# Second block's tokens in reverse order, and the keys of both blocks in one matrix, in a two-layer hybrid decoder kernel

## The chip, the cores and the metric

The kernel runs on one core of one Trainium2 chip. The metric is the device time of one execution in microseconds (us); the time before is the median of three runs. A profiled execution is one more run, with the hardware profiler on; all rows below are from it. The engines are named as the profile names them: PE is TensorE's matmuls, PEld its weight loads, DVE is VectorE, ACT is ScalarE, POOL is GpSimd, SP is SyncE.

## The reference

The input is 256 tokens of width 1024, all in fp32. Layer 0 mixes the tokens with a gated linear recurrence, HGRN2, of 8 heads of 128; layer 1 mixes them with attention. Each is followed by a SwiGLU network of width 2816, each sub-layer has an RMS norm ahead of it and a residual add behind it, and a last RMS norm closes the trunk.

```python
# layer 0, per head: S_t = diag(f_t) S_{t-1} + (1 - f_t) i_t^T ; o_t = S_t^T q_t
q = jax.nn.silu(q); f = lbf + (1.0 - lbf) * jax.nn.sigmoid(fz); k = 1.0 - f
...
diff = cum[:, :, :, None, :] - cum[:, :, None, :, :]          # cum: running sum of log f
decay = jnp.exp(jnp.where(causal[:, :, None], diff, -jnp.inf))
scores = jnp.einsum('bhtn,bhsn,bhtsn->bhts', qb, kb, decay)
...
# layer 1 (256 tokens are one block, so every query sees its own block, causally)
s_own = jnp.einsum('bhqd,bhpd->bhqp', qb, kown).astype(f32) * scale + bias_own
s_own = jnp.where(dist_own >= 0, s_own, -jnp.inf)
```

The weight of key s in query t is a product of the gates f between them, feature by feature, so it is no single matrix product. `bias_own` is a table looked up by the bucket of the distance between query and key.

## The kernel before

**Weights and activations in two parts.** A product of fp32 accuracy is made of three products in TensorE's single-pass format fp32r: weight and activation are each split in a high and a low part (hi = rounded, lo = the rest), and hi·hi, lo·hi and hi·lo are summed in PSUM (`mm_w`, `mm_x`). Weights come from HBM in 206 loads (line 399, issued from SP's queue) into a ring of six buffers `raw`; ScalarE writes `whi` (line 410) and VectorE writes `wlo` (line 412), each into a ring of six pieces of up to 1024 columns. Products whose operands aren't split are fp32 matmuls, which stand as two records each in the trace. Every `mm` is recorded with the helper's line 453.

**Order.** The order of instructions on each engine is made by a planner (`Order`) when the program is built: each step has an engine, an estimated cost, a due time and the steps that it needs. TensorE's main stream, the products with weights, is written out in order; the small matmuls of the heads ("T" steps) are put into it where the planner believes their inputs to have been ready for 1500 ns. The hardware's semaphores then make sure of the real order.

**The heads of layer 0.** The class `Core` does one head: `forget` makes the gates f, `query` makes q, and `step(m)` for m = 1, 2, 4 ... 64 builds the tree of products of gates: at level m, the tokens stand in pairs of runs of m, and the queries of each second run are multiplied with the product of the gates of their run so far (`Q[2m]`), the keys of each first run with the product of what follows them (`K[2m]`). With m from 2 to 32, each has one multiplication on VectorE (lines 848 and 853; 840 for the first queries) and a copy of the untouched half on ScalarE (850, 855; 843). `scores` then multiplies keys and queries level by level on TensorE: at level m, keys of the first runs meet queries of the second runs. The 256 tokens are two blocks of 128 (index a). For m = 4, 8 and 16, `level` makes one fp32 matmul for each block: the block's whole key matrix `K[m]` of 128 less m columns is the stationary operand, and the 64 queries of the second runs are the moving one. Level 32 and level 64 share two matmuls (`both`), for which the copies on lines 862 and 864 bring the operands together; one more (`k128`, `q128`) joins the two blocks. `s0` does level 2 and the diagonal's neighbours, and a product with `ones128` the diagonal. VectorE copies the blocks that count from PSUM to the score matrix `pm`, by a mask (`take`, line 890, and `s0e`, line 912), and ScalarE those of the large levels (`far`, lines 941 to 945). `values` multiplies `pm` with the values.

**The bias table.** Behind the heads, one fp32 matmul of 33 rows and 384 columns (`tbr`, `oh`) spreads the table of biases over distances; the result goes to DRAM (`scr`), and 8 DMAs on POOL's queue (line 1012) bring it back as `bt`, one row of 256 biases per query and head, read in layer 1's attention (`attend`). The POOL queue also makes the inverse norms (`ny`, line 609).

## Time and profile before

| | us |
|---|---|
| median of 3 runs | 619.15 |
| the runs | 618.98 to 620.29 |
| the profiled execution | 618.95 |
| its span, first to last instruction | 617.2 |
| PE busy | 609.3 (99%) |
| PEld busy | 589.1 (95%) |
| DVE busy | 441.9 (72%) |
| ACT busy | 361.4 (59%) |

Busy time is the time that at least one instruction of the engine was under way. Matmuls are pipelined, so a single matmul's duration in a timeline is longer than what it adds to the time; that is read from the distances between the starts. The granted clock of TensorE is 0.997 of full speed over the execution.

### The profile page before, as it was taken

How to read it: one execution, taken by the hardware profiler on the slowest of the kernel's cores; microseconds unless marked ns; L12 is line 12 of the kernel's file. 1: busy time of each engine (PE TensorE's matmuls, PEld its weight loads, DVE VectorE, ACT ScalarE, POOL GpSimd, SP SyncE). 2: the span in 40 equal slices, each digit the busy share in tenths (PEclk: the TensorE clock that was granted, in tenths of full speed). 3: DMA queues.
4: the chain of work that ended last, by engine and by line, in shares of the span. 5: the costliest groups of instructions: out<-in, count | busy, mean ns of one | idle time of the engine just before them, and what ended most of it. 6: DMA issues, size and time to landing. Idle time of an engine off the chain costs nothing.

```text
span 617.2 us, 12450 instructions
## 1 busy us (share of the span) xinstructions
PE 609.3 (99%) x4856; PEld 589.1 (95%) x4856; DVE 441.9 (72%) x798; ACT 361.4 (59%) x705; POOL 45.8 (7%) x84
## 2 busy tenths in 40 slices
PE   9999999999999999999999999999999999999995
PEld 7899999999999999999998899999999999999995
DVE  6899888869676666666669678877686666666654
ACT  7798887857554444444447566655674444444443
POOL 0042223201300000000000000000100000000003
PEclk9999999999999999999999999999999999999998
DMA  8856534443985555555563564446645666555501
GB/s 308 326 172 197 172 104 142 143 162 116 224 290 202 180 199 198 186 198 198 182 202 118 217 212 148 161 138 204 202 151 196 204 202 184 190 189 178 184 2 69
DMA packets 32951, 111.82 MB, mean 181 GB/s; under 512 B 4395, under 2 KB 5836, under 8 KB 32892
## 3 DMA queue, kind: packets, MB, share of 16 engines
q1 hardware_dynamic: 31340, 108.82, 53.3%
q0 software_dynamic: 448, 1.25, 1.0%
q10 hardware_dynamic: 1104, 0.95, 0.6%
q8 instruction: 38, 0.62, 0.4%
q14 instruction: 21, 0.17, 0.1%
HBM read 109.76 MB, written 1.25 MB: 180 GB/s over the span
## 4 chain that ended last, share of the span: by engine, by line
PE 99%; DVE 0%; ACT 0%; issue 0%; POOL 0%; POOLq 0%; ACTq 0%
PE psB L453 49%; PE psA L453 49%; PE psB L1169 0%; PE psB L1215 0%; PE psA L614 0%; DVE fw L1268 0%; ACT raw L1279 0%; DVE raw L1246 0%; PE psB L614 0%; ACT sq L1249 0%; POOL ident masks.py:199 0%; DVE fa L1273 0%; POOL ident masks.py:197 0%; DVE fz L1274 0%; DVE fz L1270 0%
## 5 line engine op out<-in xcount | busy, mean ns | idle before, releaser
L412 DVE TENSOR_TENSOR wlo<-raw,whi 128x1024 fp32r<-128x1024 f32 (+1 forms) x208 | 248.9, 1206 | 105.8 <-ACT whi L410 105.5
L410 ACT ACTIVATE whi<-raw 128x1024 fp32r<-128x1024 f32 (+1 forms) x207 | 213.9, 1046 | 143.9 <-issue 66.2
L453 PE MATMUL psB<-xh,whi 128*128 128x256 f32 x608 | 171.2, 285 | 0.0
L453 PE MATMUL psB<-xh,wlo 128*128 128x256 f32 x608 | 166.6, 277 | 0.0
L453 PE MATMUL psB<-xl,whi 128*128 128x256 f32 x608 | 162.3, 278 | 0.0
L453 PE MATMUL psA<-xh,whi 128*128 128x256 f32 x544 | 150.3, 280 | 0.0
L453 PE MATMUL psA<-xh,wlo 128*128 128x256 f32 x544 | 148.7, 277 | 0.0
L453 PE MATMUL psA<-xl,whi 128*128 128x256 f32 x544 | 144.0, 277 | 0.0
L453 PEld LDWEIGHTS psB<-xh,wlo 128*128 128x128 f32 x608 | 114.5, 188 | 0.8
L453 PEld LDWEIGHTS psB<-xh,whi 128*128 128x128 f32 x608 | 114.5, 188 | 0.8
L453 PEld LDWEIGHTS psB<-xl,whi 128*128 128x128 f32 x608 | 111.4, 188 | 0.0
L453 PEld LDWEIGHTS psA<-xh,whi 128*128 128x128 f32 x544 | 102.2, 188 | 0.6 <-issue 0.5
L453 PEld LDWEIGHTS psA<-xh,wlo 128*128 128x128 f32 x544 | 102.3, 188 | 0.0
L453 PEld LDWEIGHTS psA<-xl,whi 128*128 128x128 f32 x544 | 99.3, 188 | 0.0
L453 PE MATMUL psB<-hl,whi 128*128 128x256 f32 x160 | 44.2, 276 | 0.0
L453 PE MATMUL psB<-hh,whi 128*128 128x256 f32 x160 | 44.2, 276 | 0.0
L453 PE MATMUL psB<-hh,wlo 128*128 128x256 f32 x160 | 44.2, 276 | 0.0
L1028 ACT ACTIVATE u<-sgq 128x256 f32<-128x256 f32 x44 | 18.0, 409 | 36.9 <-DVE sgq L1026 36.7
L453 PE MATMUL psA<-whi,hl 128*128 128x512 f32 (+1 forms) x96 | 36.0, 375 | 0.0
L453 PE MATMUL psA<-wlo,hh 128*128 128x512 f32 (+1 forms) x96 | 35.8, 373 | 0.0
L453 PE MATMUL psA<-whi,hh 128*128 128x512 f32 (+1 forms) x96 | 35.5, 370 | 0.0
L453 PEld LDWEIGHTS psB<-hh,whi 128*128 128x128 f32 x160 | 30.0, 188 | 0.0
(192 smaller groups left out, 807.3 us busy)
## 6 DMA issues: line engine op xcount, KB each, us to landing
raw<-in_w_dram SPq DMA_DIRECT2D x202, 512.0 KB, 3.5
hT<-in_x_dram SPq DMA_DIRECT2D x8, 128.0 KB, 5.3
raw<-in_w_dram SPq DMA_DIRECT2D x4, 256.0 KB, 4.3
bt<-scr POOLq DMA_DIRECT2D x8, 128.0 KB, 7.8
out_dram<-raw SPq DMA_DIRECT2D x2, 320.0 KB, 2.3
bt<-in_final_dram ACTq DMA_DIRECT2D x1, 512.0 KB, 5.3
out_dram<-raw ACTq DMA_DIRECT2D x2, 192.0 KB, 2.3
scr<-be POOLq DMA_DIRECT2D x1, 192.0 KB, 2.5
```

Source lines behind the costliest of these rows:

```text
L410: od.op("A", ca(n), lambda h=h, r=r, o=o, n=n: A.activation(h[:, :n], r[:, o:o + n], AF.Copy), reads=[r], alloc=[h], due=due)
L412: od.op("V", cv(n), lambda h=h, lo=lo, r=r, o=o, n=n: V.tensor_tensor(lo[:, :n], r[:, o:o + n], h[:, :n].bitcast(FT), op=OP.subtract), rea ...
L453: T.matmul(o, a, b, start=start, stop=stop, skip_group_check=True)
L1028: od.op("A", ca(S), lambda: A.activation(sg.tile, gs.tile, AF.Sigmoid), reads=[gs], alloc=[sg], due=due)
```

## The change

Three things are changed.

**The order of tokens.** The host puts tokens 128 to 255 in reverse order, for all of the kernel, and turns the output back. In the second block, the earlier run of each pair then stands second. Two helpers, `first` and `second`, pick the earlier and later runs of both blocks in one access (`cut` writes the access pattern out), and the masks follow.

**Keys of both blocks in one matrix.** At each level only the keys of the earlier runs are wanted, 64 in each block of 128. In the reversed order those of the second block stand where the first block has those that aren't wanted, so the two sets fill one matrix of 128 columns without moving a key to another row of the scores. The decayed keys are kept in one buffer `kk` in place, and ScalarE gathers from it the 128 columns of `K[2m]` at each level. `level` becomes one fp32 matmul with 128 stationary and 128 moving columns, and levels 32 and 64 use it too; the copies of lines 862 and 864 go, `last` has three activations for four, `far` has seven for five.

**The bias table in the reversed order.** It has 640 columns for 384, made by four fp32r matmuls of 33 rows from a split table; `bt` has three blocks of 128 biases for each head, brought back by 18 DMAs on POOL's queue: 2 of 64 partitions and 16 of 16 partitions, in runs of 128 floats where runs of 256 floats were. So that it fits, `so`, `xsf`, `q128`, `k128` and `pm`, which had tiles of their own, now lie inside `bt`'s tile.

```diff
+NOH = 640
...
-    bt = new("bt", [P, NH * S])
+    bt = new("bt", [P, NH * 3 * P])
...
+    def inside(tag, c0, n, bufs):
+        turn = [0]
+        def make():
+            turn[0] += 1
+            c = c0 + n * ((turn[0] - 1) % bufs)
+            return bt.tile[:, c:c + n]
+        rings[tag] = Ring(make, bufs)
+        return c0 + n * bufs
+    at = inside("so", 0, S, 3)
+    at = inside("xsf", at, S, 3)
+    at = inside("q128", at, P, 2)
+    at = inside("k128", at, P, 2)
+    pm_at = at
...
-    oh = fixed("oh", [33, 384])
+    oh = fixed("oh", [33, NOH])
...
-    pms = [fixed(f"pm{i}", [P, 3, P]) for i in range(2)]
+    pms = [Buf(None) for _ in range(2)]
+    for i, t in enumerate(pms):
+        t.tile = bt.tile[:, pm_at + 3 * P * i:pm_at + 3 * P * i + 3 * P].rearrange("p (a t) -> p a t", a=3)
...
-            self.K = {m: new(f"k{m}", [P, S], 2) for m in (2, 4, 8, 16, 32, 64)}
+            self.K = {m: new(f"k{m}", [P, S], 2) for m in (2, 4, 8, 16, 32)}
+            self.K[64], self.kk = new("k128", [P, P], 2), new("k64", [P, S], 2)
...
-                od.op("V", cv(P), lambda: V.tensor_tensor(v4(kn)[:, :, 0], v4(k)[:, :, 0], bc(1), op=OP.mult),
-                      reads=[k, tot], alloc=[kn], due=due)
-                o = od.op("A", ca(P), lambda: A.activation(v4(kn)[:, :, 1], v4(k)[:, :, 1], AF.Copy), reads=[k],
-                          writes=[kn], due=due + .1)
-                o.deps.append(kn.writers[0])
-                if m == 32:
-                    v2 = lambda t: t.tile.rearrange("p (a x) -> p a x", a=2)
-                    od.op("A", ca(64), lambda: A.activation(v2(k)[:, :, 96:128], v2(kn)[:, :, 0:32], AF.Copy), reads=[kn],
-                          writes=[k], due=due + .2)
-                    od.op("A", ca(P), lambda: A.activation(
-                        q.tile.rearrange("p (a y z x) -> p a y z x", a=2, y=2, z=2)[:, :, :, 0],
-                        v2(qn)[:, :, 64:128].rearrange("p a (y x) -> p a y x", y=2), AF.Copy), reads=[qn], writes=[q],
-                        due=due + .2)
...
+                kk, kn = self.kk, K[2 * m]
+                if m == 2:
+                    od.op("V", cv(P), lambda: V.tensor_tensor(first(kk, m), first(k, m), bc(1), op=OP.mult),
+                          reads=[k, tot], alloc=[kk], due=due)
+                    o = od.op("A", ca(P), lambda: A.activation(second(kk, m), second(k, m), AF.Copy), reads=[k],
+                              writes=[kk], due=due + .1)
+                    o.deps.append(kk.writers[0])
+                else:
+                    od.op("V", cv(P), lambda: V.tensor_tensor(first(kk, m), first(kk, m), bc(1), op=OP.mult),
+                          reads=[kk, tot], writes=[kk], due=due)
+                od.op("A", ca(P), lambda: A.activation(
+                    kn[:, :P].rearrange("p (b z i) -> p b z i", z=2, i=2 * m),
+                    cut(kk, 0, (4 * m, 32 // m), (P + 2 * m, 2), (1, 2 * m)), AF.Copy), reads=[kk], alloc=[kn], due=due + .2)
                 return
...
-            self.q128, self.k128 = q, k = new("q128", [P, P], 2), new("k128", [P, P], 2)
-            Q, K = Q[64], K[64]
+            self.q128 = q = new("q128", [P, P], 2)
+            Q, k = Q[64], self.kk
             def last():
-                A.activation(q[:, 64:], Q[:, 192:], AF.Copy, scale=tot[:, 2:3])
-                A.activation(q[:, :64], Q[:, P:192], AF.Copy)
-                A.activation(k[:, :64], K[:, :64], AF.Copy, scale=tot[:, 1:2])
-                A.activation(k[:, 64:], K[:, 64:P], AF.Copy)
-            od.op("A", 4 * ca(64) + 186, last, reads=[Q, K, tot], alloc=[q, k], due=due)
+                A.activation(q[:, :64], Q[:, P:192], AF.Copy, scale=tot[:, 3:4])
+                A.activation(q[:, 64:], Q[:, 192:], AF.Copy)
+                A.activation(k[:, :64], k[:, :64], AF.Copy, scale=tot[:, 1:2])
+            od.op("A", 3 * ca(64) + 186, last, reads=[Q, k, tot], writes=[k], alloc=[q], due=due)
...
+            def take(m, src):
+                d = ((2 * m, 64 // m), (1, m))
+                V.copy_predicated(cut(pm, m, (S - m, 2), *d), cut(mk, moff[m], (64, 2), (m, 64 // m), (1, m)), src)
             def level(b, c, m):
-                o = Q[m].tile.rearrange("p (a b z m) -> p a b z m", a=2, z=2, m=m)[:, :, :, 1]
-                for a in range(2):
-                    mm(b[:P - m, c + 64 * a:c + 64 * a + 64], K[m][:, a * P:a * P + P - m], o[:, a], start=True, stop=True)
+                mm(b[:, c:c + P], K[m][:, :P], second(Q[m], m), start=True, stop=True)
...
             for i, m in enumerate((4, 8, 16)):
-                o = od.op("T", 2 * ct(64), lambda m=m, i=i: level(b, P * i, m), reads=[K[m], Q[m]], due=due,
+                o = od.op("T", ct(P), lambda m=m, i=i: level(b, P * i, m), reads=[K[m], Q[m]], due=due,
                           **(dict(writes=[b]) if i else dict(alloc=[b])))
                 o.deps += [o1] if i else []
                 o1 = o
...
-            b3 = bank("A")
-            def both():
-                for a in range(2):
-                    c = slice(a * P, a * P + P)
-                    mm(b3[:, c], K[32][:, c], Q[32][:, c], start=True, stop=True)
-            o2 = od.op("T", 2 * ct(P), both, reads=[K[32], Q[32]], alloc=[b3], due=due)
-            o3 = od.op("T", ct(P), lambda: mm(b3[:, 2 * P:3 * P], self.k128.tile, self.q128.tile, start=True, stop=True),
-                       reads=[self.k128, self.q128], writes=[b3], due=due)
-            o3.deps.append(o2)
+            b3, o1 = bank("A"), None
+            for i, m in enumerate((32, 64)):
+                o = od.op("T", ct(P), lambda m=m, i=i: level(b3, P * i, m), reads=[K[m], Q[m]], due=due,
+                          **(dict(writes=[b3]) if i else dict(alloc=[b3])))
+                o.deps += [o1] if i else []
+                o1 = o
+            o3 = od.op("T", ct(P), lambda: mm(b3[:, 2 * P:3 * P], self.kk[:, :P], self.q128.tile, start=True, stop=True),
+                       reads=[self.kk, self.q128], writes=[b3], due=due)
+            o3.deps.append(o1)
...
             def far():
-                v = b3[:, :2 * P].rearrange("p (a x) -> p a x", a=2)
-                w = b3[:, :2 * P].rearrange("p (a y z x) -> p a y z x", a=2, y=2, z=2)[:, :, :, 0]
-                to = pm[:, 0:3:2, 64:128].rearrange("p a (y x) -> p a y x", y=2)
-                A.activation(pm[0:32, 0:3:2, 32:64], v[0:32, :, 32:64], AF.Copy)
-                A.activation(pm[64:96, 0:3:2, 96:128], v[64:96, :, 96:128], AF.Copy)
-                A.activation(to[32:64], w[32:64], AF.Copy)
-                A.activation(to[0:32], w[96:128], AF.Copy)
+                for r, n, a, t, c in ((0, 32, 0, 32, 0), (64, 32, 0, 96, 32), (32, 32, 2, 0, 64), (96, 32, 2, 64, 96),
+                                      (0, 64, 0, 64, P), (64, 64, 2, 0, 192)):
+                    A.activation(pm[r:r + n, a, t:t + n], b3[r:r + n, c:c + n], AF.Copy)
                 A.activation(pm[:, 1, :], b3[:, 2 * P:3 * P], AF.Copy)
-            od.op("A", 680, far, reads=[b3], writes=[pm], due=due)
+            od.op("A", 1500, far, reads=[b3], writes=[pm], due=due)
...
+    first = lambda b, m: cut(b, 0, (P + m, 2), (2 * m, 64 // m), *[(1, m)][:m - 1])
+    second = lambda b, m: cut(b, m, (P - m, 2), (2 * m, 64 // m), *[(1, m)][:m - 1])
...
-    scr = dr.tile([P, 384], FT, name="scr")
...
-    e = new("be", [P, 384])
-    eb = bank("B")
-    tbr = new("tbr", [33, P])
-    od.op("A", ca(P), lambda: A.activation(tbr.tile.rearrange("b (h r) -> b h r", r=REP),
-                                           tb.tile.unsqueeze(2).to_broadcast([33, NH, REP]), AF.Copy),
-          reads=[tb], alloc=[tbr], due=80)
-    od.op("T", ct(384), lambda: mm(eb[:, :384], tbr.tile, oh.tile, start=True, stop=True), reads=[tbr, oh], alloc=[eb], due=80)
-    od.op("A", ca(384), lambda: A.activation(e.tile, eb[:, :384], AF.Copy), reads=[eb], alloc=[e], due=80)
-    od.op("G", 1000, lambda: G.dma_start(scr, e.tile), reads=[e], writes=[scr_b], nbytes=196608, due=80)
-    for a in range(P // REP):
-        od.op("G", 1000, lambda a=a: G.dma_start(
-            bt[REP * a:REP * a + REP, :].rearrange("p (h s) -> p h s", h=NH),
-            bass.AP(tensor=scr.tensor, offset=scr.offset + 127 - REP * a, ap=[[383, REP], [REP * 384, NH], [1, S]])),
-            reads=[scr_b], writes=[bt], nbytes=131072, due=90)
+    e = new("be", [P, NOH])
+    ebs = bank("B"), bank("B")
+    tbh, tbl, ohr = new("tbh", [33, P], 1, FR), new("tbl", [33, P], 1, FR), new("ohr", [33, NOH], 1, FR)
+    many = tb.tile.unsqueeze(2).to_broadcast([33, NH, REP])
+    heads = lambda t: t.rearrange("b (h r) -> b h r", r=REP)
+    od.op("A", ca(P), lambda: A.activation(heads(tbh.tile), many, AF.Copy), reads=[tb], alloc=[tbh], due=80)
+    od.op("V", cv(P), lambda: V.tensor_tensor(heads(tbl.tile), many, heads(tbh.tile.bitcast(FT)), op=OP.subtract),
+          reads=[tb, tbh], alloc=[tbl], due=80)
+    od.op("A", ca(NOH), lambda: A.activation(ohr.tile, oh.tile, AF.Copy), reads=[oh], alloc=[ohr], due=80)
+    for eb, c0, n in zip(ebs, (0, 384), (384, NOH - 384)):
+        def biases(eb=eb, c0=c0, n=n):
+            mm(eb[:, :n], tbh.tile, ohr[:, c0:c0 + n], start=True)
+            mm(eb[:, :n], tbl.tile, ohr[:, c0:c0 + n], stop=True)
+        od.op("T", 500, biases, reads=[tbh, tbl, ohr], alloc=[eb], due=80)
+        al = dict(writes=[e]) if c0 else dict(alloc=[e])
+        od.op("A", ca(n), lambda eb=eb, c0=c0, n=n: A.activation(e[:, c0:c0 + n], eb[:, :n], AF.Copy), reads=[eb],
+              due=80, **al)
+    od.op("G", 1000, lambda: G.dma_start(scr, e.tile), reads=[e], writes=[scr_b], nbytes=4 * P * NOH, due=80)
+    heads3 = lambda r, n, j: bt[r:r + n, :].rearrange("p (h j s) -> p h j s", h=NH, j=3)[:, :, j]
+    rows = lambda off, step, n: bass.AP(tensor=scr.tensor, offset=scr.offset + off, ap=[[step, n], [REP * NOH, NH], [1, P]])
+    for r in range(0, P, 64):
+        od.op("G", 1000, lambda r=r: G.dma_start(heads3(r, 64, 1), rows(r, 1, 64)), reads=[scr_b], writes=[bt],
+              nbytes=262144, due=90)
+    for r in range(0, P, REP):
+        for j, off in ((0, 255), (2, 511)):
+            od.op("G", 1000, lambda r=r, j=j, off=off: G.dma_start(heads3(r, REP, j), rows(off - r, NOH - 1, REP)),
+                  reads=[scr_b], writes=[bt], nbytes=65536, due=90)
...
-        parts = ((0, slice(0, P), slice(h * S + P, h * S + S)), (1, slice(P, 384), slice(h * S, h * S + S)))
+        parts = ((0, slice(0, P), slice(h * 384, h * 384 + P)), (1, slice(P, 384), slice(h * 384 + P, h * 384 + 384)))
...
-    for i in range(384):
...
+    for i in range(NOH):
+        dist = 255 - i if i < 384 else i - 511
...
```

## Rows read from the trace of the kernel before

**Rows 1.** the profile's page: span, busy engines, the chain that ended last

```profile
span 617.2 us, 12450 instructions
...
PE 609.3 (99%) x4856; PEld 589.1 (95%) x4856; DVE 441.9 (72%) x798; ACT 361.4 (59%) x705; POOL 45.8 (7%) x84
...
PE 99%; DVE 0%; ACT 0%; issue 0%; POOL 0%; POOLq 0%; ACTq 0%
```

**Rows 2.** waits of TensorE over the whole span: us in total, times, longest

```profile
PE psA L453 <- POOL ident masks.py:199: 1.4, 1, 1.4
```

**Rows 3.** timeline of TensorE near 108 us: start us, us, line, operation

```profile
108.15 0.28 PE L453 MATMUL psB<-xl,whi 128*128 128x256 f32 x1
108.27 0.39 PE L453 MATMUL psA<-q,k 128*128 128x128 f32 x2
...
108.61 0.28 PE L453 MATMUL psB<-xh,wlo 128*128 128x256 f32 x1
108.73 0.28 PE L453 MATMUL psB<-xl,whi 128*128 128x256 f32 x1
108.85 0.54 PE L453 MATMUL psA<-q,k 128*124 128x64 f32 x4
...
109.40 0.28 PE L453 MATMUL psB<-xh,wlo 128*128 128x256 f32 x1
```

**Rows 4.** the same timeline near 101 us

```profile
101.08 0.28 PE L453 MATMUL psB<-xl,whi 128*128 128x256 f32 x1
101.19 0.38 PE L453 MATMUL psA<-q,ones 128*128 128x128 f32 x2
101.41 0.53 PE L453 MATMUL psA<-q,k 128*120 128x64 f32 x4
...
101.96 0.28 PE L453 MATMUL psB<-xh,wlo 128*128 128x256 f32 x1
```

**Rows 5.** the same timeline near 115 us

```profile
114.81 0.28 PE L453 MATMUL psB<-xl,whi 128*128 128x256 f32 x1
114.92 0.51 PE L453 MATMUL psA<-q,k 128*112 128x64 f32 x4
...
115.45 0.28 PE L453 MATMUL psB<-xh,wlo 128*128 128x256 f32 x1
```

**Rows 6.** a group of matmuls, 30 to 130 us: count, busy us, mean ns

```profile
L453 PE MATMUL psA<-q,k 128*124 128x64 f32 x32 | 4.3, 258 | 0.0
```

**Rows 7.** the same timeline near 149 us

```profile
148.44 0.28 PE L453 MATMUL psA<-xh,wlo 128*128 128x256 f32 x1
148.65 0.91 PE L453 MATMUL psB<-oh,tbr 33*128 33x384 f32 x2
...
149.71 0.29 PE L453 MATMUL psA<-xh,wlo 128*128 128x256 f32 x1
```

**Rows 8.** groups of ScalarE (ACT), 30 to 140 us: busy us, mean ns

```profile
L855 ACT ACTIVATE k<-k 128x128 f32<-128x128 f32 x40 | 12.2, 305 | 0.0
...
L862 ACT ACTIVATE k<-k 128x64 f32<-128x64 f32 x8 | 1.9, 242 | 0.0
...
L941 ACT ACTIVATE pm<-psA 32x64 f32<-32x64 f32 x8 | 1.7, 210 | 6.3 <-PE psA L453 5.9 <-DVE pm L890 0.4
```

**Rows 9.** busy time of each engine from 69 to 117 us

```profile
69.00:117.00 48.00, 48.00 (x413) 47.66 (x413) 40.42 (x103) 40.58 (x137) 11.85 (x28) 1.00 0.38 125
```

**Rows 10.** instructions on tile hT: ns min/median/max, first and last start us

```profile
L557 ACT ACTIVATE xh<-hT,pv x32: 491/494/512, 3.6 to 431.7; 128x256 fp32r<-128x256 f32 x32
...
L536 SPq DMA_DIRECT2D hT<-in_x_dram x8: 328/431/730, 0.7 to 10.1; - x8
```

**Rows 11.** line 399's loads, issue to landing, 150 to 172 us

```profile
DMA to landing us min/median/max: 4.7/10.1/13.2
```

**Rows 12.** the same, 180 to 260 us

```profile
DMA to landing us min/median/max: 3.1/3.3/4.3
```

**Rows 13.** timeline of ScalarE near 171 us, in brackets what ended its idle time

```profile
171.15 1.07 ACT L410 ACTIVATE whi<-raw 128x1024 fp32r<-128x1024 f32 x1 [0.34 <-PE psA L453]
```

More of the change, by code (lines that the diff above doesn't have):

```diff
@@ L312, in hybrid_trunk, with cut @@
     rings = {}
+    def cut(b, off, *dims):
+        t = b.tile if hasattr(b, "ring") else b
+        return bass.AP(tensor=t.tensor, offset=t.offset + off, ap=[list(t.ap[0])] + [list(d) for d in dims])
     def ring(tag, shape, bufs, dt=FT):
@@ L775, in forget @@
             k1, k2 = self.k1, self.K[2]
-            fz = lambda z: f.tile.rearrange("p (t z) -> p z t", z=2)[:, z]
-            od.op("A", ca(P), lambda: A.activation(k1[:, :P], fz(0), AF.Identity, scale=-1.0, bias=1.0), reads=[f],
-                  alloc=[k1], due=7)
-            od.op("A", ca(P), lambda: A.activation(k2.tile.rearrange("p (t z) -> p z t", z=2)[:, 1], fz(1), AF.Identity,
-                                                   scale=-1.0, bias=1.0), reads=[f], alloc=[k2], due=7)
+            od.op("A", ca(P), lambda: A.activation(k1[:, :P].rearrange("p (a t) -> p a t", a=2), first(f, 1), AF.Identity,
+                                                   scale=-1.0, bias=1.0), reads=[f], alloc=[k1], due=7)
+            od.op("A", ca(P), lambda: A.activation(second(k2, 1), second(f, 1), AF.Identity, scale=-1.0, bias=1.0),
+                  reads=[f], alloc=[k2], due=7)
             for m in (1, 2, 4, 8, 16, 32):
@@ L843, in step @@
[L843 to L845 removed]
+                    of = lambda z: cut(q, 64 * z, (448 - P * z, 2), (2, 32), (1, 2))
                 else:
                     q, qn = Q[m], Q[2 * m]
[L848 to L849 removed]
@@ L857, in step @@
[L857 to L867 removed]
+                    of = lambda z: (first, second)[z](q, m)
@@ new lines, in step @@
+                od.op("V", cv(P), lambda: V.tensor_tensor(second(qn, m), of(1), bc(0), op=OP.mult), reads=[q, tot],
+                      alloc=[qn], due=due)
+                o = od.op("A", ca(P), lambda: A.activation(first(qn, m), of(0), AF.Copy), reads=[q], writes=[qn],
+                          due=due + .1)
+                o.deps.append(qn.writers[0])
+                kk, kn = self.kk, K[2 * m]
[8 more added lines that the diff above has]
+                          reads=[kk, tot], writes=[kk], due=due)
@@ L913, in s0e @@
                                   mk[:, :2 * P].rearrange("p (a z x) -> p a z x", a=2, z=2), v)
-            od.op("V", cv(P), lambda: take(b0, 0, 2, 192), reads=[b0, mk], writes=[pm], due=due)
+            od.op("V", cv(P), lambda: take(2, cut(b0, 64, (192, 2), (2, 32), (1, 2))), reads=[b0, mk], writes=[pm], due=due)
             b, o1 = bank("A"), None
             for i, m in enumerate((4, 8, 16)):
-                o = od.op("T", 2 * ct(64), lambda m=m, i=i: level(b, P * i, m), reads=[K[m], Q[m]], due=due,
+                o = od.op("T", ct(P), lambda m=m, i=i: level(b, P * i, m), reads=[K[m], Q[m]], due=due,
                           **(dict(writes=[b]) if i else dict(alloc=[b])))
@@ L920, in scores @@
                 o1 = o
-                od.op("V", cv(P), lambda m=m, i=i: take(b, P * i, m), reads=[b, mk], writes=[pm], due=due)
-            od.op("T", ct(P), lambda: mm(b0[:, :384].rearrange("p (a x) -> p a x", a=2)[:, :, :64], ones128,
-                                         ev[:, :P].rearrange("p (a x) -> p a x", a=2), start=True, stop=True),
-                  reads=[ev], writes=[b0], due=due)
+                od.op("V", cv(P), lambda m=m, i=i: take(m, cut(b, P * i, (64, 2), (m, 64 // m), (1, m))), reads=[b, mk],
+                      writes=[pm], due=due)
@@ L925, in scores @@
+            od.op("T", ct(P), lambda: mm(cut(b0, 0, (320, 2), (1, 64)), ones128, ev[:, :P].rearrange("p (a x) -> p a x", a=2),
+                                         start=True, stop=True), reads=[ev], writes=[b0], due=due)
             od.op("V", cv(S), s0e, reads=[b0, mk], writes=[pm], due=due)
-            b3 = bank("A")
-            def both():
-                for a in range(2):
-                    c = slice(a * P, a * P + P)
-                    mm(b3[:, c], K[32][:, c], Q[32][:, c], start=True, stop=True)
@@ L1331, in _constants @@
     pair = np.arange(64)[None]
-    m = [np.concatenate([s == 2 * pair, s // 2 == pair] * 2, axis=1).astype(np.float32)]
+    m = [np.concatenate([s == 2 * pair, s // 2 == pair, s // 2 == pair, s == 2 * pair + 1], axis=1).astype(np.float32)]
     for lv in LEVELS:
-        t = np.arange(P).reshape(-1, 2, lv)[:, 1].reshape(1, -1)
-        ok = ((s // (2 * lv)) == (t // (2 * lv))) & ((s // lv) % 2 == 0)
-        m.append(np.tile(ok.astype(np.float32), (1, 2)))
+        block = np.arange(64)[None] // lv
+        m += [((s // (2 * lv) == block) & ((s // lv) % 2 == a)).astype(np.float32) for a in range(2)]
     return onehot, np.concatenate(m, axis=1).astype(np.uint8)
```

68 lines of the change are left out of this document (24 added, 44 removed).

## The prediction

> **What bounds the kernel now.** Read first the page's engines and its chain: TensorE is under way for 609.3 of 617.2 us, and the chain that ended last is 99% TensorE [rows 1]. A busy TensorE need not be one without waits, so its list of waits comes next: over the whole span it holds one wait, 1.4 us for the identity matrix at the start [rows 2]. So the time is the sum of what TensorE's instructions add to its stream, and an edit counts by the TensorE time that it takes out or puts in, or by a wait that it creates. Busy durations don't give that sum, since matmuls overlap; distances between starts do. In the timeline, products with split weights follow each other at 0.12 us (108.61 to 108.73) [rows 3]. The work of VectorE and ScalarE is hidden as long as they keep ahead: from 69 to 117 us, in the heads, they are busy 40.42 and 40.58 of 48 us, with the granted clock at 1.00, the 2.4 GHz level [rows 9].
>
> **The change, part by part.** The sum is made against the profiled execution: 618.95 us, that is a span of 617.2 and 1.75 us around it, which nothing here touches. The three runs' median is 0.20 above it, and I add that at the end.
>
> *Merged levels 4, 8 and 16.* A small group's price is the distance from the last regular product before it to the second one behind it, less two regular steps of 0.12. One fp32 matmul of 128 stationary and 128 moving columns: 108.15 to 108.61, 0.46 - 0.24 = 0.22 us. The two 64-column matmuls of level 4 (four records): 108.73 to 109.40, 0.67 - 0.24 = 0.43 [rows 3]. Level 8 stands behind a 128-column one: 101.08 to 101.96, 0.88 - 0.24 - 0.22 = 0.42 [rows 4]. Level 16: 114.81 to 115.45, 0.64 - 0.24 = 0.40 [rows 5]. So a matmul with 64 moving columns costs 0.20 to 0.215 us, nearly what one with 128 costs; and as the price falls from level 4 to 16 while the stationary matrix shrinks from 124 to 112 columns and the moving one stays at 64, I read the stationary side as what sets it. The pair becomes one 128 by 128 matmul, for which I take 0.22. Its moving operand has short runs, as the pairs' had, and they didn't make those dearer. Per head: 0.43 + 0.42 + 0.40 - 3 x 0.22 = 0.59 us. There are 8 heads (32 records of level 4, four a head [rows 6]), so 8 x 0.59 = 4.7 us off TensorE's stream. Bounds: if moving columns set the price, the merged matmul costs what the pair cost and nothing is saved; at the cheapest row, 0.20, it is 8 x (1.25 - 0.60) = 5.2.
>
> A rule of the Trainium skill speaks against this part: "TensorE: Matmul & The Clock Gate", section "Back-to-back issue gap", gives about 60 cycles for a matmul of up to 64 columns and 134 for one of 128, so two halves would cost no more than the whole and the gain would be nil. The rows just read, 0.22 for the whole against 0.40 to 0.43 for two halves, disagree, for these fp32 matmuls with a fresh stationary matrix each.
>
> *Levels 32 and 64.* Two 128 by 128 matmuls before (`both`), two after (`level` twice): nothing on TensorE. `s0`, the diagonal, the product of the blocks and `values` keep their number and shapes.
>
> *The bias product.* Its fp32 matmul spans 148.44 to 149.71, 1.27 - 0.24 = 1.03 us [rows 7]. After: two fp32r products of 384 columns and two of 256. With 0.12 for 256 columns and half as much again for 384, 2 x 0.18 + 2 x 0.12 = 0.60, so 0.4 us off. As no row shows an fp32r product of 33 rows, I bound it from 0 to 0.6.
>
> *ScalarE and VectorE in the heads.* On VectorE the number and size of instructions stay. ScalarE: five copies of the untouched keys a head (305 ns each), with line 862 (242, 64 columns) and line 864 (128 columns, so some 305), become one such copy and five gathers; `last` loses one 64-column copy (about 242); `far` has six small activations of at most 64 columns for four, and its smallest takes 210 now [rows 8]. That is 5 x 305 + 242 + 305 against 6 x 305, then 242 less, then at most 2 x 210 more: about -60 ns a head, so nothing. The heads' stage is 5% shorter for TensorE (0.59 of some 11.9 us: 72 regular steps of 0.12, the 1.25 above, and nine more units of 128 columns at 0.22), which lifts both engines from 84% to some 89% of it [rows 9]. Their cover is the stock of split weights, below.
>
> *The added waits.* The next level's multiplication writes `kk` in place, so it waits on VectorE until ScalarE has gathered from `kk`; behind it stand the other steps of the heads and the weight splits of line 412. Before, it waited for ScalarE's copy of the other half, which is as long a step [rows 8]. Chain for chain: one multiplication and one ScalarE copy a level, before and after. I take 0, and from -0.1 to +3 us for the whole, as priced in the rivals. Four kinds of buffers now share one tile. One tile's slices don't wait for each other here: `hT` is loaded in 8 parts until 10.1 us, and ScalarE reads its first part at 3.6 [rows 10]. So 0 for that too.
>
> *POOL's queue and the bias table.* 18 DMAs for 8, 1.5 MB for 1.05, in 3072 runs of 512 B for 1024 runs of 1 KB. POOL has nothing else that is urgent but `ny`, which the planner puts ahead by its due time. What the DMAs disturb are the weights: loads issued from 150 to 172 us take 10.1 us to land (13.2 at most), against 3.3 later [rows 11, 12]. Still TensorE doesn't feel it, since at 171.15 us the split of the next weights waits for TensorE to give a buffer back [rows 13]: the ring is full. Five of six pieces ahead are 5 x 8 x 3 x 0.12 = 14 us of products; less some 3.5 us for a split (1.07 on ScalarE [rows 13], about as much on VectorE, and the waits between), landing may be some 10 us later still before TensorE runs dry. By bytes (1.5 times the delay of 13.2 - 3.3 = 9.9) landing is 5 us later, by runs (3 times) 20 later. I take the former's side: 0; the latter is the slower rival.
>
> "DMA: Bandwidth & Descriptors", section "How a descriptor splits into AXI transactions", in the Trainium skill, has a transfer that starts off a 256 B boundary pay for one more partial transaction; for runs of 512 B in place of 1 KB that would make my estimate some 1.7 times the delay in place of 1.5, which the 10 us still cover. No row shows such runs.
>
> Sum: 618.95 - 4.7 - 0.4 = 613.85, and with the 0.20 to the median **614.0 us**.
>
> **The rivals.**
>
> *Nothing gained by merging.* If moving columns set a merged matmul's price, only 0.4 us goes: 619.15 - 0.4 = 618.7. For it: no row has a 128-column moving operand in runs of 4 to 16 elements. Against it: the prices read in [rows 3 to 5]. 6%. The page on TensorE named above would give this one.
>
> *Waits in the heads.* The planner puts a small matmul where it believes the inputs ready; with VectorE and ScalarE at 89% it may be wrong more often. Ahead of the bias product TensorE already starts 148.65 - 148.44 - 0.12 = 0.09 us late [rows 7]. Nine such groups a head, 8 heads, at 0.09 are 6.5 us at worst; at half of them 3 us, 614.0 + 3 = 617. For it: the longer queue on two engines. Against it: not one wait of TensorE there now [rows 2]. 12%.
>
> *The biases' DMAs starve the weights (slower).* If the delay of the weight loads goes by runs, landing is 20 us later than now where 10 are covered, so TensorE stands still for some 10 us at about 175 to 190 us: 614.0 + 10 = 624. It decides from the point where the delay of 9.9 us doubles. For it: landing rose from 3.3 to 13.2 us with an eighth of a MB at a time and only 8 of them. Against it: bytes rise only 1.5 times, and 18 issues spread over a longer time, in which the weights take their turns. 8%.
>
> **How the numbers follow.** The forecast has 70%, the three rivals 6, 12 and 8%, and 4% goes to a larger gain than summed (5.2 and 0.6: 613.3). Bounds of the forecast's own terms: 613.3 to 614.4. The range reaches up to the waits' 617.0, which takes in the second rival and leaves out the first and the third, 14%; below it goes to 612.9, the larger gain less the 0.2 by which runs differ and rounding. A measurement here can tell 0.2% (1.2 us) from no change, so faster means under 617.9: 70 + 12 + 4 = 86%; same 6%; slower 8%.
>
> **What would show it.** In the changed profile: TensorE's list of waits still holds the start's 1.4 us alone; level 4, 8 and 16 have 16 records each of 128 by 128 and 128 moving columns in place of 32, and a lone one spans 0.46 us between its neighbours' starts; the bias product spans some 0.85; `values` of a head come some 11.3 us behind those of the head before where some 11.9 were; weight loads around 150 to 180 us take longer to land, under 24 us, and splits still wait for TensorE. I'm wrong if the lone merged matmul spans 0.65 us (first rival), if short idle times show on TensorE before small matmuls of the heads (second), or if TensorE waits for `wlo` past 170 us (third).

## The result and the profile after

The changed kernel takes **614.79 us** (median of 4 runs, 613.86 to 615.27) against 619.07 of the kernel before beside it: a ratio of 0.9927, with a 95% interval from 0.9907 to 0.9946. The forecast was 614.0, with a range from 612.9 to 617.0. The profiled execution took 614.85 us. Five more runs of the unaltered kernel on another occasion gave 614.43 (ratio 0.9924, 0.9911 to 0.9936).

The page of the changed kernel, its span, the busy engines and the chain that ended last, the same lines as [rows 1]:

```profile
span 613.1 us, 12295 instructions
...
PE 605.2 (99%) x4810; PEld 585.4 (95%) x4810; DVE 440.5 (72%) x799; ACT 361.7 (59%) x707; POOL 47.1 (8%) x94
...
PE 99%; DVE 0%; ACT 0%; issue 0%; POOL 0%; POOLq 0%; ACTq 0%
```

TensorE is still all of the chain, and busy 4.1 us less, as the span is shorter by 4.1. Its list of waits answers to [rows 2] and is the same: the start alone (the helper's line 453 is now 459).

```profile
PE psA L459 <- POOL ident masks.py:199: 1.4, 1, 1.4
```

**The merged matmuls.** The group of the levels from 4 to 32 in the heads, count, busy us and mean ns: 64 records are 4 levels of 8 heads with two records each, all 128 by 128.

```profile
L459 PE MATMUL psA<-q,k 128*128 128x128 f32 x64 | 11.9, 274 | 0.0
```

A lone one in the timeline of TensorE (start us, duration us, line, operation), to be read as [rows 3]:

```profile
106.59 0.28 PE L459 MATMUL psB<-xl,whi 128*128 128x256 f32 x1
106.70 0.38 PE L459 MATMUL psA<-q,k 128*128 128x128 f32 x2
...
107.04 0.28 PE L459 MATMUL psB<-xh,wlo 128*128 128x256 f32 x1
```

From 106.59 to 107.04 are 0.45 us; less two regular steps of 0.12 that is 0.21, where 0.22 was taken.

**The bias product**, which answers to [rows 7], in the timeline of TensorE:

```profile
154.50 0.39 PE L459 MATMUL psA<-xl,whi 128*128 128x256 f32 x2
154.81 0.44 PE L459 MATMUL psB<-ohr,tbh 33*128 33x384 f32 x1
155.09 0.34 PE L459 MATMUL psB<-ohr,tbl 33*128 33x384 f32 x1
155.27 0.29 PE L459 MATMUL psB<-ohr,tbh 33*128 33x256 f32 x1
155.40 0.28 PE L459 MATMUL psB<-ohr,tbl 33*128 33x256 f32 x1
155.60 0.39 PE L459 MATMUL psA<-xh,whi 128*128 128x256 f32 x1
155.83 0.28 PE L459 MATMUL psA<-xh,wlo 128*128 128x256 f32 x1
```

The first row stands for two products, at 154.50 and, one regular step later, at 154.62. From there to 155.83 are 1.21 us, less 0.24: 0.97, or 0.99 with the starts to the nanosecond. From the first of the group's four starts on, the distances are 0.28, 0.18, 0.13 and, to the product behind, 0.20; that one takes 0.23 to the next instead of 0.12. In the middle of the group the columns cost what the forecast took, 0.18 and 0.12; what was not foreseen lies at both ends.

**The sum.** Taken in the same way over every small group from 38 to 166 us, with the starts to the nanosecond and a regular step of 0.118, the small groups cost 28.78 us before and 23.97 after: 4.81 us less, of which the bias product is 1.03 - 0.99 = 0.04 and the heads 4.8. The span fell by only 4.1. Of the 0.7 between them 0.5 is at the start, where this profile fell that much behind the one of before; the other 0.2 is in the regular steps between the groups. In the timeline of TensorE just behind the first weights, the changed kernel in its first profile:

```profile
6.10 1.05 PE L459 MATMUL psB<-whi,xl 128*128 128x512 f32 x2
6.95 0.86 PE L459 MATMUL psB<-wlo,xh 128*128 128x512 f32 x2
7.66 0.63 PE L459 MATMUL psB<-whi,xh 128*128 128x512 f32 x2
```

and in a second profile, of its other set of runs:

```profile
6.66 0.62 PE L459 MATMUL psB<-wlo,xh 128*128 128x512 f32 x2
7.12 0.62 PE L459 MATMUL psB<-whi,xh 128*128 128x512 f32 x2
```

The products are the same in both; in the first its last row (`whi`, `xh`) stands 0.54 us later. From 6.10 to 6.95, two products of 512 columns take 0.85 us, 0.43 each; behind these rows it is 0.23. So the first products run at about half of the later pace, and for how long differs between executions. Half the pace would be the 1.2 GHz level, but the granted clock doesn't show it: it reads 1.00, the 2.4 GHz level, in this very stretch of the changed kernel's first profile (columns as in [rows 9]):

```profile
5.00:7.00 2.00, 2.00 (x6) 1.53 (x6) 1.78 (x3) 1.79 (x4) 0.00 (x0) 1.00 0.96 322
```

So the cause of the slow start stays open; only its length is measured. The second profile's span is 612.5, 4.7 below the 617.2 of before.

**What covers it.** Busy time from 66 to 112 us in the heads, in the order of [rows 9], ScalarE's the fourth:

```profile
66.00:112.00 46.00, 46.00 (x394) 45.73 (x393) 40.16 (x108) 41.70 (x141) 11.56 (x34) 1.00 0.45 143
```

VectorE is busy 40.16 and ScalarE 41.70 of 46 us, 87 and 91%, where some 89% was forecast. And the weights' loads issued between 160 and 182 us, while the bias table is brought back (us from issue to landing, as in [rows 11]), with ScalarE's waits for loads from 150 to 200 us (in total, times, longest):

```profile
DMA to landing us min/median/max: 4.7/14.6/17.0
```

```profile
ACT whi L416 <- DMA raw<-in_w_dram: 9.9, 6, 2.9
```

They take up to 17.0 us where 13.2 were the most before, and six splits now wait for their load where none did. None of it reaches TensorE.

### The profile page after: what moved, and what is told of

The parts are those of the page before. It is cut to its first block, busy times and chain, and to the rows that moved or that the text cites. A ratio compares the mean times of both kernels' runs of the same rounds, so it can differ in the third digit from the quotient of the medians.

```text
span 613.1 us, 12295 instructions
## 1 busy us (share of the span) xinstructions
PE 605.2 (99%) x4810; PEld 585.4 (95%) x4810; DVE 440.5 (72%) x799; ACT 361.7 (59%) x707; POOL 47.1 (8%) x94
## 4 chain that ended last, share of the span: by engine, by line
PE 99%; DVE 0%; ACT 0%; issue 0%; POOL 0%; POOLq 0%; ACTq 0%
PE psB L459 50%; PE psA L459 48%; PE psB L1192 0%; PE psB L1238 0%; PE psA L637 0%; DVE fw L1291 0%; ACT raw L1302 0%; DVE raw L1269 0%; PE psB L637 0%; ACT sq L1272 0%; POOL ident masks.py:199 0%; DVE fa L1296 0%; POOL ident masks.py:197 0%; DVE fz L1297 0%; DVE fz L1293 0%
## 6 DMA issues: line engine op xcount, KB each, us to landing
bt<-scr POOLq DMA_DIRECT2D x2, 256.0 KB, 11.3
```

## The experiments

All ratios are to the kernel before on the same chip, which took 618.99 to 619.15 us in these sets of runs. A difference to the changed kernel is one to 614.79, unless another time is named. Each kernel is the changed one with one edit, but for the stacked table, which takes a second step from the bias product over the whole array, and the run of the unaltered kernel. The planner orders each of them anew. The edits are shown in short.

### One part undone: two matmuls a level again

```diff
 def level(b, c, m):
+    if m < 32:
+        for a in range(2):
+            mm(b[:P, c + 64 * a:c + 64 * a + 64], K[m][:, :P],
+               cut(Q[m], m + a * (P - m), (2 * m, 64 // m), (1, m)), start=True, stop=True)
+        return
     mm(b[:, c:c + P], K[m][:, :P], second(Q[m], m), start=True, stop=True)
...
-                o = od.op("T", ct(P), lambda m=m, i=i: level(b, P * i, m), reads=[K[m], Q[m]], due=due,
+                o = od.op("T", 2 * ct(64), lambda m=m, i=i: level(b, P * i, m), reads=[K[m], Q[m]], due=due,
```

> The changed kernel with levels 4, 8 and 16 each made by two fp32 matmuls of 64 moving columns again (48 in place of 24), on the merged key matrix of 128 stationary columns; nothing else differs. Theory (the stationary matrix sets the price, so a half costs what the whole costs): each half takes 0.22 us of TensorE's stream, the time rises by 24 x 0.22 = 5.2 us, to about 620.0, and a pair spans 0.67 us between its neighbours' starts. Rival (moving columns set the price): a half takes 0.11, the time stays at 614.8. Rival (the gain came from elsewhere, from shorter queues on ScalarE and VectorE): the time rises by well under 5 us.

Measured: 620.69 us, ratio 1.0028 (1.0016 to 1.0040). The pair in its timeline of TensorE:

```profile
80.16 0.28 PE L459 MATMUL psB<-xl,whi 128*128 128x256 f32 x1
80.28 0.55 PE L459 MATMUL psA<-q,k 128*128 128x64 f32 x4
...
80.84 0.28 PE L459 MATMUL psB<-xh,wlo 128*128 128x256 f32 x1
```

80.16 to 80.84: 0.68 - 0.24 = 0.44 us, twice the merged matmul's price. The time is 5.9 us above the changed kernel's, of which 24 x 0.22 = 5.3 are these matmuls. So the whole gain goes when the merging alone is undone; the reversed order, the shorter queues and the bias table account for none of it. The remaining 0.6 us is one group at 118 us, which costs 1.37 us where its like costs 0.67; TensorE waits there for VectorE (0.4 us in its list of waits). The time is also 1.7 us above the kernel before: that wait is in it, and some 0.7 us because the pairs' stationary matrix now has 128 columns, at 0.44 to 0.45 a pair, where the kernel before had 112 to 124, at 0.40 to 0.43.

### Which side sets a small matmul's price

Four kernels change the size of the operands of levels 4, 8 and 16 and leave out the scores that then lack an operand; VectorE's masked copies of these levels keep their number and take what is there.

```diff
+    half = cut(Q[m], m, (2 * m, 64 // m), (1, m))          # the first block's 64 queries
+    mm(b[:P, c:c + 64], K[m][:, :P], half, ...)            # half moving
+    mm(b[:64, c:c + P], K[m][:, :64], second(Q[m], m), ...)   # half stationary
+    mm(b[:64, c:c + 64], K[m][:, :64], half, ...)          # both half
+    mm(b[:72, c:c + P], K[m][:, :72], second(Q[m], m), ...)   # 72 stationary columns
```

> The changed kernel, but levels 4, 8 and 16 multiply only the first block's 64 queries (64 moving, 128 stationary columns, one matmul); the scores of the second block's queries at these levels are left out (those of the first block stand there). Theory (stationary columns set the price below 128 moving ones): nothing changes, 614.8, a lone one still spans 0.46 us between its neighbours' starts. Rival (moving columns set it): 24 x 0.11 = 2.6 us less, 612.2, and a span of 0.35.

Measured: 614.75 us, ratio 0.9934 (0.9920 to 0.9949). In the timeline:

```profile
77.54 0.28 PE L459 MATMUL psB<-xl,whi 128*128 128x256 f32 x1
77.66 0.33 PE L459 MATMUL psA<-q,k 128*128 128x64 f32 x2
...
77.99 0.28 PE L459 MATMUL psB<-xh,wlo 128*128 128x256 f32 x1
```

0.45 - 0.24 = 0.21 us: half of the moving columns and the same price. The table in "TensorE: Matmul & The Clock Gate", section "Back-to-back issue gap", in the Trainium skill, by which a matmul of up to 64 columns takes less than half of one with 128, doesn't hold for these. The section gives that table for a matmul by itself and says that in a stream of weight loads and matmuls both set the spacing; the unchanged 0.21 us goes with that.

> The changed kernel, but levels 4, 8 and 16 have only the first 64 key columns as stationary operand (64 stationary, 128 moving); the scores of the other 64 key rows at these levels are left out. Theory in the form that the dearer of the two sides sets the price: nothing changes, 614.8, span 0.46. If the stationary side alone sets it: 24 x 0.11 = 2.6 us less, 612.2, span 0.35.

Measured: 622.39 us, ratio 1.0052 (1.0035 to 1.0069), dearer by 7.6 us where nothing or a gain was expected. In the timeline:

```profile
81.19 0.28 PE L459 MATMUL psB<-xl,whi 128*128 128x256 f32 x1
81.40 0.43 PE L459 MATMUL psA<-q,k 128*64 128x128 f32 x2
...
81.99 0.29 PE L459 MATMUL psB<-xh,wlo 128*128 128x256 f32 x1
```

81.19 to 81.99: 0.80 - 0.24 = 0.56 us. The matmul starts 0.21 behind the product before it where 0.12 is regular, and both it and the next product hold up what follows. The rows of the weight loads (PEld) show what is late: the first one is of the changed kernel and belongs to the lone matmul shown above, the other two are of this kernel, the matmul's own and that of the product behind.

```profile
106.59 0.30 PEld L459 LDWEIGHTS psA<-q,k 128*128 128x128 f32 x2
```

```profile
81.40 0.19 PEld L459 LDWEIGHTS psA<-q,k 128*64 128x64 f32 x2
81.76 0.19 PEld L459 LDWEIGHTS psB<-xh,whi 128*128 128x128 f32 x1 [0.17 <-issue]
```

With 128 columns the load starts together with the product ahead (106.59) and so a step before its own matmul (106.70). With 64 it starts 0.21 us behind the product ahead, and its matmul with it (81.40); the load of the product behind starts as late, 0.20 us after the small matmul's second record. Neither is hidden under the product before it.

> The changed kernel, but levels 4, 8 and 16 multiply the first 64 key columns with the first block's 64 queries alone (64 stationary, 64 moving); three quarters of these levels' scores are left out. Theory (the dearer side sets the price): the price halves, 24 x 0.11 = 2.6 us less, 612.2, span 0.35. Rival (a fixed cost of each fp32 matmul sets it): nothing changes, 614.8.

Measured: 619.79 us, ratio 1.0014 (1.0004 to 1.0023). In the timeline:

```profile
80.09 0.28 PE L459 MATMUL psB<-xl,whi 128*128 128x256 f32 x1
80.30 0.33 PE L459 MATMUL psA<-q,k 128*64 128x64 f32 x2
...
80.78 0.28 PE L459 MATMUL psB<-xh,wlo 128*128 128x256 f32 x1
```

80.09 to 80.78: 0.69 - 0.24 = 0.45 us. So the numbers of theory and rival were missed by both of these kernels, in the same way: with 64 stationary columns, 0.45 and 0.56 can be read as 0.11 and 0.22, the price by the dearer side, and 0.34 more in both. No run shows 64 by 64 without that addition. The whole runs agree: 24 x (0.56 - 0.22) = 8.2 against 7.6 measured, 24 x (0.45 - 0.22) = 5.5 against 5.0.

> The changed kernel, but levels 4, 8 and 16 have the first 72 key columns as stationary operand (64 took 0.56 us, 112 to 128 took 0.20 to 0.22), with 128 moving; the scores of the other 56 key rows at these levels are left out. Theory (the added cost belongs to operands that fit half of the array): with 72 columns it is gone, a lone matmul takes 0.22 and the time is 614.8. Rival (any stationary operand below the full array pays, by how much is missing): some 0.5 us each, 24 x 0.28 = 6.7 us more, 621.5.

Measured: 614.04 us, ratio 0.9916 (0.9902 to 0.9931). In the timeline:

```profile
77.11 0.28 PE L459 MATMUL psB<-xl,whi 128*128 128x256 f32 x1
77.23 0.38 PE L459 MATMUL psA<-q,k 128*72 128x128 f32 x2
...
77.57 0.28 PE L459 MATMUL psB<-xh,wlo 128*128 128x256 f32 x1
```

0.46 - 0.24 = 0.22 us: with 72 stationary columns the added cost is gone. It doesn't grow with what is missing; it is there at 64 and not at 72.

A rule of the Trainium skill would fit: by "TensorEngine Tiling (Array Packing)", section "Key Properties", a change of the tiling mode drains TensorE. Whether operands of 64 columns count as such a mode here, though the kernel asks for none, isn't shown: no record names a drain. The runs show the late loads and their size, 0.34 us for going there and back.

### The bias product over the whole array

```diff
-    oh = fixed("oh", [33, NOH])
-    tb = fixed("tb", [33, NH])
-    V.memset(tb[32:33, :], MASKED)
+    oh = fixed("oh", [P, NOH])
+    tb = fixed("tb", [P, NH])
+    G.memset(oh.tile, 0.0)
+    G.memset(tb.tile, 0.0)
+    G.memset(tb[32:33, :], MASKED)
...
-    tbh, tbl, ohr = new("tbh", [33, P], 1, FR), new("tbl", [33, P], 1, FR), new("ohr", [33, NOH], 1, FR)
+    tbh, tbl, ohr = new("tbh", [P, P], 1, FR), new("tbl", [P, P], 1, FR), new("ohr", [P, NOH], 1, FR)
```

> The changed kernel, but the bias product has 128 rows in place of 33, the added 95 rows being zeros on both sides; the same four fp32r matmuls of 384, 384, 256 and 256 columns. In the changed kernel that group takes 0.99 us where 0.60 were expected, and with 64 stationary columns a matmul took 0.33 us more than its columns, 128 or 64, account for. Theory (a product that uses half of the array's rows or columns pays some 0.35 us for going there and back): the group takes 0.60 to 0.65 us, and the time is 614.4, too near to 614.8 to be told by the clock alone. Rival (a cost of fp32r after fp32, or of a new kind of matmul): the group stays at 0.99.

Measured: 614.30 us, ratio 0.9923 (0.9907 to 0.9940). In the timeline, the group with a product ahead (four in its row, the last at 153.63 + 3 x 0.12 = 153.99) and behind:

```profile
153.63 0.62 PE L459 MATMUL psA<-xl,whi 128*128 128x256 f32 x4
154.09 0.34 PE L459 MATMUL psB<-ohr,tbh 128*128 128x384 f32 x1
154.27 0.33 PE L459 MATMUL psB<-ohr,tbl 128*128 128x384 f32 x1
154.44 0.28 PE L459 MATMUL psB<-ohr,tbh 128*128 128x256 f32 x1
154.56 0.28 PE L459 MATMUL psB<-ohr,tbl 128*128 128x256 f32 x1
...
154.79 0.28 PE L459 MATMUL psA<-xh,wlo 128*128 128x256 f32 x1
```

153.99 to 154.79: 0.80 - 0.24 = 0.56, or 0.59 with the exact starts: 128 rows in place of 33, and 0.40 us cheaper. The steps are 0.18, 0.17, 0.12 and 0.11 with nothing added at the ends. The first weight load of the group, in the changed kernel and here:

```profile
154.81 0.18 PEld L459 LDWEIGHTS psB<-ohr,tbh 33*128 33x128 f32 x1
```

```profile
153.97 0.19 PEld L459 LDWEIGHTS psB<-ohr,tbh 128*128 128x128 f32 x1
```

With 33 rows it starts together with its matmul (154.81), with 128 a step ahead (154.09). The load of the product behind does the same: at 155.60 with its matmul there, at 154.56 here, a step ahead of its matmul at 154.67. So the 33 rows paid for going there and back like the 64 columns, and the same two loads start with their matmuls in the kernel before, too (148.65 and 149.49): its 1.03 us can be read as 384 columns at 0.22 for each 128, 0.66, and 0.37 more.

The time, 0.5 us below the changed kernel's, can't be told from this gain, and in the profile the gain doesn't last. The regular step behind the group is 0.118 us up to about 170 us, where the changed kernel's is 0.113 (between 162 and 168 us 54 matmuls are under way here and 56 there, at a granted clock of 1.00 in both), and this takes the 0.40 us back. Why the step differs stays open.

### The two parts of the table stacked

With the array filled anyway, the table's high part can stand in rows 0 to 32 and its low part in rows 64 to 96.

```diff
+    # tb and oh are loaded a second time, into rows 64 to 96; tbh[64:97] becomes the low part
-            mm(eb[:, :n], tbh.tile, ohr[:, c0:c0 + n], start=True)
-            mm(eb[:, :n], tbl.tile, ohr[:, c0:c0 + n], stop=True)
+            mm(eb[:, :n], tbh.tile, ohr[:, c0:c0 + n], start=True, stop=True)
```

> The changed kernel with the bias product made over all rows of the array, and the high part of the table in rows 0 to 32 and its low part in rows 64 to 96 against the same one-hot matrix twice, so that two fp32r matmuls (384 and 256 columns) do what four did. With 33 rows the four took 0.99 us, with 128 rows 0.59. Theory (the cost of leaving the full array is gone, columns set the rest): the group takes 0.28 to 0.35 us and the time falls by 0.65 us against the changed kernel, to about 614.1. Rival (the product's cost is hidden or fixed): the group stays above 0.5.

Measured: 614.57 us, ratio 0.9924 (0.9911 to 0.9938). In the timeline (three products in the first row, the last at 154.68 + 2 x 0.12 = 154.92):

```profile
154.68 0.51 PE L459 MATMUL psA<-xl,whi 128*128 128x256 f32 x3
155.03 0.46 PE L459 MATMUL psB<-ohr,tbh 128*128 128x384 f32 x2
...
155.44 0.28 PE L459 MATMUL psA<-xh,wlo 128*128 128x256 f32 x1
```

154.92 to 155.44: 0.52 - 0.24 = 0.28, 0.295 with the exact starts, as expected of the group. The time was expected 0.65 us lower and isn't: beside it the changed kernel took 614.43. Here too the regular step behind the group is 0.118 us in place of 0.113, and some 0.5 of the 0.7 us are gone by 171 us.

> The changed kernel itself, unaltered, beside the run with the stacked bias product on the same chip: 614.8, with the start of the profiled execution and the 0.7% gain against the kernel before to be seen a second time. The first profile of it lost about 0.5 us in its first 10 us against the profile of the kernel before; if that belongs to the change, it is there again, if it is chance, it isn't.

Measured: 614.43, as told above; the late start isn't there again, so it doesn't belong to the change.

### The transfers that disturb the weights, three times

```diff
-    for r in range(0, P, 64):
+    for r in [0, 64] * 3:
...
-    for r in range(0, P, REP):
+    for r in [*range(0, P, REP)] * 3:
```

> The changed kernel with each of the 18 DMAs that bring the bias table back issued three times, with the same content. This prices the third rival, the weights starved by those DMAs. In the changed kernel loads land up to some 14 us after issue, and the split weights' lead over TensorE falls from 11 to 8 us. Theory (the stock is used up in proportion to the disturbance): three times the disturbance uses more than the stock of raw and split weights, and TensorE stands still, 620 to 635 us. Rival (the transfers take turns and the weights keep nearly their rate): no wait of TensorE, 614.8.

Measured: 617.50 us, ratio 0.9976 (0.9967 to 0.9986): 2.7 above the changed kernel, below the theory's 620 and above the rival's 614.8. TensorE's added waits (in total, times, longest), and us from issue to landing of the weights' loads issued between 205 and 250 us:

```profile
PE psA L459 <- DVE wlo L418: 1.1, 2, 0.9
PE psB L459 <- DVE wlo L418: 0.6, 1, 0.6
```

```profile
DMA to landing us min/median/max: 12.1/16.9/18.1
```

The expectation's 14 us are those of loads issued up to 172 us; with 18 DMAs the most is the 17.0 above. The loads of the row take up to 18.1 us, those issued from 182 to 200 us 17.5 to 19.8: hardly more. What grows is how long that lasts: with 18 DMAs those issued from 200 to 260 us take 5.4 at most. The waits for `wlo` fall between 240 and 262 us, some 60 us after such landings began. So with three times the transfers the third rival sets in, and costs 2.7 us, not 10.

### More work for ScalarE in the heads

```diff
+    if m == 32:
+        for _ in range(5):
+            t = new("more", [P, P], 2)
+            od.op("A", ca(P), lambda t=t: A.activation(t.tile, self.k1[:, :P], AF.Copy), reads=[self.k1],
+                  alloc=[t], due=due)
```

> The changed kernel with five more copies of 128 columns on ScalarE in each head, read by nobody: 5 x 0.2 = 1.0 us a head on an engine that is busy 43.66 of 48 us there. This prices the second rival, waits in the heads. Theory (the planner puts the small matmuls later and the stock of split weights covers the rest): 614.8, no wait of TensorE. Rival (the heads are at the limit of ScalarE, each added us shows): up to 8 us more, 618 to 623.

Measured: 618.36 us, ratio 0.9989 (0.9980 to 0.9999): 3.6 us above the changed kernel, in the rival's range; the theory of no wait failed. A copy took 0.30 us, not 0.2, and ScalarE is busy 6.8 us more over the whole (368.5 against 361.7). TensorE's added waits, and the busy time from 66 to 112 us:

```profile
PE psA L459 <- ACT xh L580: 1.7, 1, 1.7
...
PE psA L459 <- DVE mov L854: 0.6, 1, 0.6
PE psB L459 <- DVE xl L977: 0.3, 1, 0.3
```

```profile
66.00:112.00 46.00, 46.00 (x393) 45.73 (x392) 38.21 (x103) 43.44 (x158) 12.05 (x32) 1.00 0.39 127
```

ScalarE is at 43.44 of 46 us, 94%, and TensorE still doesn't stand idle in this stretch. The longest wait comes behind the heads: 1.7 us for the first split of layer 0's next input (`xh`), the end of a line from the last head's result over its norm to the residual. The other two come in the last heads, at 116 and 136 us. So up to 112 us the planner keeps the small matmuls' inputs ahead at this load, and most of the price comes where there's nothing left to put between. The changed kernel stands at 91% in this stretch.

## Why the prediction was right

**The merging: right, in mechanism and size.** 4.7 us were forecast for 24 merged pairs; the groups of the heads cost 4.8 less, and undoing it alone takes away all of the gain. The reading behind it, that the stationary side sets the price, is right for 64 moving columns (0.21 us against 0.21 to 0.22). It was put too simply for a smaller stationary side: at 72 columns with 128 moving the price stays at 0.22, so the dearer side sets it. The kernel before already held a sharper row: two fp32 matmuls of 128 stationary columns and a single moving one (`ones`, `sqacc`) span 135.00 to 135.68 us in its timeline, 0.68 - 0.24 = 0.44, as much as two with 64 or 128.

**The bias product: mis-sized.** The step that failed is the term "2 x 0.18 + 2 x 0.12 = 0.60" with its "0.4 us off". The price before was measured with all that lies at the group's ends, the price after was made from columns alone. The group took 0.99, and 0.04 was saved. As 0 stood in its bounds, the range was not touched. The runs showed what is at the ends: some 0.37 to 0.40 us for a product with 33 rows, whose weight load and the next one start late, gone with 128. The 0.09 us by which TensorE starts late ahead of that product, from which the second rival took its price, were this too and not a wait for inputs: with 128 rows the group starts a regular step behind the product ahead (153.97 to 154.09).

**ScalarE, VectorE and the added waits: right.** The load of both went to 87 and 91%, 89 was forecast, and TensorE got no new wait in the heads; the chain through `kk` and the shared tile cost nothing that the profile shows. The prediction's sign for this, a distance of 11.3 us between the `values` of two heads, can't be read from single heads, as the planner put the small matmuls of neighbouring heads in another order: the distances go from 6 to 15 us. Their mean fell from 10.6 to 10.0, by the forecast 0.6 from a lower level.

**POOL's DMAs: right in the outcome, not in the rule.** "By bytes 5 us later" meant 18 at most; 17.0 was measured, six splits waited for loads and TensorE for none. But three times the transfers don't follow that rule: 4.5 times the bytes of before would make landing 9.9 x 3.5 = 35 us later, and 6.6 was measured (19.8 against 13.2). TensorE then ran dry although 10 us were taken as covered. So how long the loads stay late counts here, not only how late one is, and that the sum by bytes came near for 18 DMAs was in part luck.

**The sum.** 619.07 - 4.8 = 614.3 is what the groups give; 614.79 and 614.43 were measured. Of the forecast's 614.0, the bias term's 0.4 accounts for the difference to 614.4, and what is left is within the spread of the runs (613.86 to 615.27), of which the length of the slow start alone can make half a microsecond.

**The rivals.** That merging saves nothing is refuted by the undone part and by the half moving operand. Waits in the heads did not come; with ScalarE at 94% in place of 91% short ones did, most of them behind the heads. The starved weights did not come; with three times the transfers they did, and where between one and three it begins wasn't measured.

## What to carry to other kernels

Where TensorE is all of the chain, price a small matmul by the distance between its neighbours' starts, both before and after an edit, with the same ends; a price from columns alone leaves out what it costs to get there and back. An fp32 matmul whose stationary matrix is fresh cost here what the larger of its two sides costs (72 to 128 stationary and 1 to 128 moving columns), so fill both sides: two half-filled ones merged to one were worth half of their price. And where its neighbours use the whole array, look at the weight loads of an operand of 64 columns or of 33 rows, and fill it up where they start late: 72 columns and, with zeros, 128 rows were enough here. For the columns the whole run shows it (24 matmuls, 8 us); for the one product of 33 rows only its own group does.

## What the runs showed of the hardware

- An fp32 matmul of 128 by 128 takes 0.21 to 0.22 us of the stream, one with 64 moving and 128 stationary columns the same, one with 72 stationary and 128 moving columns the same, and one with 128 stationary columns and 1 moving 0.22.
- Going to a matmul with 64 stationary columns and back costs 0.34 us on top (0.45 and 0.56 us in place of 0.11 and 0.22), one with 33 rows 0.37 to 0.40 for the group; 128 rows, 95 of them zeros, are cheaper than 33 (0.59 against 0.99 us). The first weight load then starts 0.20 to 0.21 us behind the product ahead, where a full one starts together with it; the next full load is late too.
- The first products of an execution run at about half of the later pace (0.43 us for 512 columns against 0.23) while the granted clock reads 1.00, and the end of that moved by 0.5 us between two executions of one kernel.
- Products of 256 columns follow each other at 0.113 us in some stretches and at 0.118 in others, at a granted clock of 1.00: from 162 to 168 us 0.113 in the changed kernel, 0.118 with the bias product over 128 rows.
- Transfers on POOL's queue made the weights' loads land in up to 13.2 us (8 DMAs), 17.0 (18) and 19.8 (54), where 3.3 was the median without them in the kernel before [rows 12]: three times as many lengthened the time of late landings far more than the landings.
